# A two-layer hybrid decoder trunk: the heads' stage in steps of four wide products in place of three

## The chip, the cores and the metric

The kernel runs on one core of one Trainium2 chip. The metric is the device time of one launch in microseconds (us), as a median of several runs; lower is better. One of the executions was also profiled.

The engines are named as the profile names them: PE (TensorE, matrix products and transposes), PEld (its weight loads), DVE (VectorE), ACT (ScalarE), POOL (GpSimd) and SP (SyncE, which issues the DMAs).

## The reference

Input x is 1024 positions by 1024 channels, float32. Two layers follow each other, then a final RMSNorm. A layer normalizes x, multiplies it with one wide input matrix, and splits the columns among three causal token mixers, their gates, and three merge gates.

```
proj = rmsnorm(x) @ w_in
A:  a = conv31(a_val * sigmoid(a_glu)); y_a = silu(layernorm(a)) * silu(a_z)
B:  q, k, v = silu(conv4(qkv)), 8 heads of 128; q, k l2-normed; beta, decay per head
    o = gated_delta_rule(q, k, v, beta, decay);  y_b = rmsnorm(o) * silu(b_z)
C:  y_c = gelu(c_u) * (tril(W_s) layernorm(gelu(c_v)) + b) * silu(c_z)
x = x + (g0*(y_a @ a_proj) + g1*(y_b @ b_proj) + g2*(y_c @ c_proj)) @ w_out
```

with g0, g1 and g2 the sigmoids of the merge gates. The part that matters here is B. The gated delta rule goes through the positions in chunks. Within a chunk a lower triangular matrix made of keys, decay and beta is inverted; from chunk to chunk a state S of 128 by 128 is carried on:

```
v_new = u - w @ S        (u, w: the inverse applied to values and keys)
o     = q_dec @ S + qk @ v_new
S     = d * S + k_dec^T @ v_new
```

## The kernel before

**Data.** Everything is float32. A wide product keeps float32 accuracy by splitting both factors into a high and a low part and adding three passes (high by high, high by low, low by high), each a product of 128 by 128 by 512. They write `ps` tiles. The splits are an ACT copy and a POOL or DVE subtraction (lines 184 and 185). Products of one chunk (128 by 128) run as narrow float32 products; the profile lists two records for each.

**Stages of a layer.** First come some products, then `pairs`: the input projection in a scheme with seven block products for eight. The norms, the convolutions and the first two heads' beginnings run beside it. Then comes the heads' stage, which the change touches: TensorE has 16 more gate tiles to make (`plain`, of 48 wide products each, weights loaded and split ahead), then proj_c and proj_a, and between these wide products the eight heads run. The rest of proj_c and proj_a, proj_b and the output product follow.

**The heads' stage.** `interleave(lead, sides)` takes a leading generator, `feed`, whose every step emits three wide products (one k of one half, in `product`, line 257), and a list of side generators, each with a first step and a gap. After each step of the lead it advances those sides that are due. So the order of the text is woven out of positions that are written down by hand as AT_ constants. PE, ACT and DVE run this text in its order here (`manual_schedule`); POOL's and SP's orders are chosen by a planner. A period of 32 steps (PERIOD) belongs to each head, and head s starts from o = 32 s + 17. Sides are advanced in the order of the heads, and for a head in the order of the list. The yc splits come last.

The sides of a head, with the lines of their work:

- `head_load` issues the loads of q, k, v, of the decay row `gam` and of z (lines 736 and 753).
- `head_decay` makes a mask on POOL (line 789), then eight exponentials on ACT, one a step (line 794).
- `head_keys` transposes the keys (line 762, two blocks of four), copies them (ACT, line 777) and sums eight squares (ACT, line 780).
- `head_pairs` makes q by k (line 811) and k by k (line 830) for all chunks, two blocks of four each, with DVE products behind (lines 812, 833); between them DVE makes the small vector W (lines 815 to 820) while POOL scales kE (line 823) and takes a power (line 822). Then parts go out to DRAM and come back in another shape.
- `head_sub` is a DVE solve of 15 steps, a product (line 864) and a reduction (line 865) each, and `head_fetch` loads the result.
- `head_inv` widens the inverse from blocks of 16 to 128: six sets of small products (lines 923, 930, 946, 956 with 958, 968, 974) with ACT copies between them.
- `head_values` transposes q and v, two blocks of four each; ACT sums four squares behind each q block (line 891) and scales four copies behind each v block (line 901).
- `head_rec` is the recurrence over eight chunks, three steps a chunk. One step applies the inverse (line 1004), and ACT makes `vh` (line 1006) and squares an earlier output (line 1027). The next makes the state's and the output's products (lines 1012 and 1021), and DVE the new state (line 1017) and the output (line 1023). The third multiplies the state with keys and queries (lines 995 and 1000); DVE makes `rt` (line 997) and ACT a copy (line 1001).
- `head_out` takes a power and a product on POOL (lines 1047 and 1048), waits some steps, transposes the output (line 1055), multiplies on DVE (line 1057) and stores.

The recurrence and the inversion write tiles of `pr`, of which there are two in turn; transposes and pairs write `pa`, also two. The 24 units of SBUF that hold a head's tiles are handed out first in, first out.

A gate tile, when its 48 products are done, gets two tanh on ACT (lines 1156 and 1158), which are queued when the next tile's first product is emitted, and is stored.

```
sides.append((with_priority(late(lambda s=s: head_rec(s, r.E))), o + AT_REC[0], AT_REC[1]))
...
interleave(steps(feed, n * H + RAMP + EXTRA), sides)
```

Of the kernel before, what the change touches and what calls it, by code (L numbers as in the profile page):

```python
# [18 lines left out]
NT = 8  # L19
H = 8  # L20
# [5 lines left out]
PERIOD = 32  # L26
RAMP = 17
HEAD0 = 8
AT_LOAD = -29
AT_DECAY = -32  # L30
AT_KEYS = -21
AT_PAIRS = -19, 1.4
AT_SUB = 4, 1
AT_FETCH = 19
AT_INV = -6, 1.6
AT_VALUES = -8, 2.5
AT_REC = 11, 1
AT_OUT = 8, 3
N_LATE = 3
SPLIT_AT = {8: (10, 12), 4: (3, 5)}  # L40
REST_AT = 0
# [5 lines left out]
S_HEAD = -4, 1  # L47
S_NEXT = 50, 61, 77, 76, 74
STEP_US, IDLE_US, WIDE_US = 0.7, 1.5, 1.4
EXTRA = 2  # L50
AT_YC = -20
LAG_DMA, LAG_POOL = 4, 5
B_ENG = "Activation", "DVE"
# [17 lines left out]
def hybrid_trunk_kernel(ctx: ExitStack, tc: tile.TileContext, x, norm_g, w_in, a_dw, a_dw_b,  # L71
# [104 lines left out]
    ya_d, yc_d = (dr.tile([4, P, T], F32, name=f"y{nm}_d") for nm in "ac")  # L176
# [12 lines left out]
        for _ in g:  # L189
            pass  # L190

    def interleave(lead, sides):


        sides = [[g, first, gap] for g, first, gap in sides]
        i = 0
        for _ in lead:
            for sd in list(sides):
                while sd[1] <= i:
                    if next(sd[0], sides) is sides:  # L200
                        sides.remove(sd)
                        break
                    sd[1] += sd[2]
            i += 1
        while sides:
            for sd in list(sides):
                if next(sd[0], sides) is sides:
                    sides.remove(sd)

    def steps(g, n):  # L210
        for _ in range(n):
            if next(g, n) is n:
                return
            yield

    def chain(*gs):
        for g in gs:
            yield from g
# [27 lines left out]
    def product(w, rhs, kt, done, ahead, used=None):  # L246


        ps = psums()
        for k in range(kt):  # L250
            for h in range(2):
                if 2 * k + h in SPLIT_AT[kt]:
                    ahead()
                if 2 * k + h == REST_AT and rests:
                    rests.pop()()
                for i, (wi, ri) in enumerate(PASSES):
                    pe.matmul(ps[h], lhsT=w[wi][:, k, :], rhs=rhs(h, ri, k),  # L257
                              start=(k == 0 and i == 0), stop=(k == kt - 1 and i == 2))
                if used and h:
                    used(k)  # L260
                yield
        FW(*w)
        with tc.high_priority():
            rest = done(ps)
        if rest:
            rests.append(rest)

    rests = []

    def half_first(ws, rhs, kt, parts=1):  # L270


        pss = [psums() for _ in ws]
        n = HALF // parts
        for h in range(2):
            for p in range(parts):
                sl = slice(p * n, (p + 1) * n)
                for w, ps in zip(ws, pss):
                    for k in range(kt):
                        for i, (wi, ri) in enumerate(PASSES):  # L280
                            pe.matmul(ps[h][:, sl], lhsT=w[wi][:, k, :], rhs=rhs(h, ri, k)[:, sl],  # L281
                                      start=(k == 0 and i == 0), stop=(k == kt - 1 and i == 2))
                        yield pss
        for w in ws:
            FW(*w)
# [755 lines left out]
    def head_out(l, s):  # L1041
        o, zs = by_chunk(s.u["vn"]), s.u["z"]
        f = sm.tile([P, 8], F32, name="f", bufs=1)
        dve.tensor_scalar(out=f, in0=s.ssq, scalar1=EPS, scalar2=128.0 * EPS, op0=ALU.add, op1=ALU.mult)
        dve.scalar_tensor_tensor(out=f, in0=s.sso, scalar=1.0 / 128.0, in1=f, op0=ALU.mult, op1=ALU.add)
        fr = sm.tile([P, 8], F32, name="fr", bufs=1)
        pool.tensor_tensor(out=fr, in0=f, in1=mhalf, op=ALU.pow)
        pool.tensor_tensor(out=o, in0=o, in1=bc(fr, 2, P), op=ALU.mult)
        for _ in range(LAG_POOL):
            yield  # L1050
        c = cols["ong", l]
        for half in range(2):
            tp = pa.tile([P, HALF], F32, name="pa")
            for j in range(4):
                pe.transpose(tp[:, j * P:(j + 1) * P], o[:, half * 4 + j, :], ident)
            sl = slice(half * HALF, (half + 1) * HALF)
            dve.scalar_tensor_tensor(out=zs[:, sl], in0=tp, scalar=vec[:, c:c + 1], in1=zs[:, sl],
                                     op0=ALU.mult, op1=ALU.mult)
            yield
        sp.dma_start(out=yb_d[s.hd], in_=zs)  # L1060
        F(s.u["vn"], s.u["z"])
# [143 lines left out]
    def load_split(src, ks, name, ys, lag=0, gap=0, apart=0):  # L1205

        new = []
        for k in ks:
            hi, lo = U(name + "h", dt=F32R), U(name + "l", dt=F32R)
            sp.dma_start(out=lo.bitcast(F32), in_=src[k])  # L1210
            new.append((hi, lo))
            for _ in range(apart):
                yield
        for _ in range(lag):
            yield
        for hi, lo in new:
            split(lo.bitcast(F32), hi, lo, dve)
            ys.append((hi, lo))
            for _ in range(gap):
                yield  # L1220
# [70 lines left out]
    def layer(l, before, ws=None, parts=1):  # L1291
# [4 lines left out]
        pss = []  # L1296
# [105 lines left out]
        hs = [new_head(hd) for hd in range(H)]  # L1402
# [37 lines left out]

        def plain():
            br, m = order[n_gates]
            for i, pss in enumerate(half_first((w(),), h_rhs, 8)):
                if i in (4, 6):
                    w.ahead()
                yield
            use_gate_tile(br, m)(pss[0])()
            for br, m in order[n_gates + 1:]:
                yield from product(w(), h_rhs, 8, use_gate_tile(br, m), w.ahead)
            yield from proj_c(yc, mp, w)  # L1450
            yield from proj_a(ya, mp, w)
        mp, yc, ya, yb = [], [], [], []
        w = Weights([(w_part(l, C_GATE + br * D + m * P), 8) for br, m in order[n_gates:]] +
                    [(src[l][:, m * P:(m + 1) * P], kt) for src, kt in ((c_proj, 4), (a_proj, 4), (b_proj, 8))
                     for m in range(NT)])
        feed = plain()
        n, sides = PERIOD, [(second_head, 0, S_SECOND[1])]
        def side2(f, first):
            sides.append((late(f), first, 1))
        for hd, s in enumerate(hs):  # L1460
            o = hd * n + (RAMP if hd else HEAD0)
            def side(f, first, gap=1):
                sides.append((late(f), o + first, gap))
            sides.append((with_priority(late(lambda s=s: head_rec(s, r.E))), o + AT_REC[0], AT_REC[1]))
            if hd:
                if hd > 1:
                    side(lambda s=s: head_load(s, "kq"), AT_LOAD - n)
                    side(lambda s=s: head_load(s, "d"), AT_DECAY - LAG_DMA - n)
                    side(lambda s=s: head_decay(s, r), AT_DECAY - n)
                    side(lambda s=s: head_keys(s), AT_KEYS - n)  # L1470
                    side(lambda s=s: head_pairs(s, r), AT_PAIRS[0] - n, AT_PAIRS[1])
                side(lambda s=s: head_sub(s), AT_SUB[0] - n, AT_SUB[1])
                side(lambda s=s: head_load(s, "v"), AT_VALUES[0] - 8)
            if hd:
                side(lambda s=s: head_fetch(s), AT_FETCH - n)
            side(lambda s=s: head_inv(s), *AT_INV)
            side(lambda s=s: head_values(s), *AT_VALUES)
            if hd < H - 1:
                side(lambda s=s: head_load(s, "z"), AT_OUT[0] + n - 8)
                side(lambda s=s: head_out(l, s), AT_OUT[0] + n, AT_OUT[1])  # L1480
        with tc.manual_schedule(engines={getattr(mybir.EngineType, e) for e in B_ENG}):
            plain_steps = (len(order) - n_gates) * 16
            side2(lambda: load_split(yc_d, range(4), "yc", yc, 8, 3), plain_steps + AT_YC)
            interleave(steps(feed, n * H + RAMP + EXTRA), sides)
        run(head_load(hs[H - 1], "z"))
        left = plain_steps + 2 * 8 * NT - (n * H + RAMP + EXTRA)
        interleave(feed, [(head_out(l, hs[H - 1]), 5, 2), (load_split(ya_d, range(4), "ya", ya), left - 78, 1),
                          (load_split(yb_d, range(3), "yb", yb), left - 24, 1),
                          (load_split(yb_d, range(3, H), "yb", yb, apart=2), left - 6, 1)])
        mg, wo = {}, []  # L1490
        def used(k):
            F(*yb[k])
            wf = wr_pool.tile([P, 8, P], F32, name="wr").rearrange("p k c -> p (k c)")
            sp.dma_start(out=wf, in_=w_out[l][k * P:(k + 1) * P, :])
            hi, lo = U("woh", dt=F32R), U("wol", dt=F32R)
            with tc.high_priority():
                split(wf, hi, lo, pool if k in (3, 5, 7) else dve)
            wo.append((hi, lo))
# [71 lines left out]
    with tc.manual_schedule(engines={mybir.EngineType.PE}):  # L1570
        norms, ws = first_layer()
# [5 lines left out]
        for l in range(DEPTH):  # L1577
            before = layer(l, before, ws, 1 if l else 2)
            ws = None
# [28 lines left out]
```

## Time and profile before

| what | value |
|---|---|
| median of 3 runs | 2663.96 us (2663.27 to 2668.45) |
| profiled execution | 2663.31 us |
| its span, first to last instruction | 2661.5 us |
| PE busy | 2568.4 us, 97% |
| DVE busy | 1656.7 us, 62% |
| ACT busy | 1256.4 us, 47% |
| POOL busy | 1423.5 us, 53% |
| mean granted clock of PE | 0.991 |

The profile is of one execution. Busy shares are means over stages with different limits. Times in rows are microseconds from the span's start, means marked ns are nanoseconds. "out<-in" gives the tiles that an instruction writes and reads, and the number behind it the partitions by elements. A bracket behind a row of the timeline says how long the engine was idle before it and what ended that. Records of PE overlap, since products are pipelined: the time that a product takes from the engine is read from start to start.

### The profile page before, as it was taken

What the parts mean: (1) busy time and instruction counts of PE and PEld (TensorE: products, weight loads), DVE (VectorE), ACT (ScalarE), POOL (GpSimd) and SP (SyncE); (2) the same over time, 40 slices, a digit from 0 to 9 for tenths busy, and PEclk for the clock granted to TensorE, in tenths of its full rate; (3) what the DMA queues carried; (4) which work ended last, traced back from release to release, by engine and by line L of the source; (5) the groups of instructions that cost most, each with busy time, mean ns of one, the idle gap of its engine ahead of it and who ended that gap; (6) DMA issues with size and microseconds to landing.
All of it is one profiled execution on the core that took longest, in us unless ns stands there. A gap on an engine that the chain in (4) does not pass through costs nothing.

```text
span 2661.5 us, 42685 instructions
## 1 busy us (share of the span) xinstructions
PE 2568.4 (97%) x15963; PEld 2113.4 (79%) x15963; DVE 1656.7 (62%) x2934; ACT 1256.4 (47%) x2996; POOL 1423.5 (53%) x1144
## 2 busy tenths in 40 slices
PE   7899999999899999999999999999998999999998
PEld 6688888778688888788867888887787888877887
DVE  6698999756445454445276889997564545444442
ACT  4434434565466666322134343356554666652221
POOL 7867777768433332363167777776673333324520
PEclk9999999999999999999999999999999999999999
DMA  4122333534634445554312223343445444445432
GB/s 158 48 64 88 104 95 107 155 108 122 184 103 111 145 106 169 182 170 138 107 68 63 63 82 110 95 150 104 118 131 173 114 131 112 136 139 189 156 130 76
DMA packets 361636, 319.65 MB, mean 120 GB/s; under 512 B 98931, under 2 KB 313557, under 8 KB 360405
## 3 DMA queue, kind: packets, MB, share of 16 engines
q1 hardware_dynamic: 361428, 316.92, 39.5%
q8 instruction: 126, 2.06, 0.3%
q14 instruction: 82, 0.66, 0.1%
HBM read 221.12 MB, written 95.75 MB: 119 GB/s over the span
## 4 chain that ended last, share of the span: by engine, by line
PE 80%; DVE 6%; POOL 4%; ACT 4%; DMA 3%; issue 2%; SPq 0%; DVEq 0%; POOLq 0%; ACTq 0%
PE ps L357 36%; PE ps L257 24%; PE ps L1271 7%; DMA gam<-gc_d 2%; PE pa L762 1%; PE ps L281 1%; POOL S L185 1%; PE pr L1012 1%; PE pr L1004 1%; PE pr L995 1%; POOL st L298 1%; PE pr L1021 1%; DMA wr<-in_w_in_dram 1%; PE pa L811 1%; DVE nm L1084 1%
## 5 line engine op out<-in xcount | busy, mean ns | idle before, releaser
L185 POOL TENSOR_TENSOR S<-st,S 128x512 fp32r<-128x512 f32 x248 | 332.5, 1341 | 166.1 <-ACT S L184 165.7
L695 DVE SCALAR_TENSOR_TENSOR pr<-o,dwT,pr 128x512 f32<-128x512 f32 (+7 forms) x480 | 357.0, 745 | 10.6
L357 PE MATMUL ps<-hT,A 128*128 128x512 f32 x1488 | 363.5, 392 | 0.0
L185 POOL TENSOR_TENSOR wl<-wr,wh 128x512 fp32r<-128x512 f32 (+2 forms) x164 | 198.6, 1225 | 293.1 <-PE ps L257 138.7
L257 PE MATMUL ps<-hT,wh 128*128 128x512 f32 x960 | 334.4, 429 | 0.0
L373 DVE TENSOR_TENSOR o<-o,ps 128x512 f32<-128x512 f32 x430 | 286.2, 681 | 77.4 <-PE ps L357 66.2
L357 PEld LDWEIGHTS ps<-hT,A 128*128 128x128 f32 x1488 | 279.4, 189 | 58.5 <-issue 0.5
L184 ACT ACTIVATE S<-st 128x512 fp32r<-128x512 f32 x248 | 156.7, 632 | 338.3 <-PE ps L357 196.4
L185 POOL TENSOR_TENSOR A<-wr,A 128x512 fp32r<-128x512 f32 x186 | 253.0, 1361 | 22.3 <-ACT A L184 22.0
L695 DVE SCALAR_TENSOR_TENSOR pr<-o,cvT,pr 128x512 f32<-128x512 f32 (+3 forms) x288 | 213.1, 752 | 48.9 <-ACT pr L715 43.3
L257 PE MATMUL ps<-hT,wl 128*128 128x512 f32 x480 | 189.3, 394 | 0.0
L184 ACT ACTIVATE A<-wr 128x512 fp32r<-128x512 f32 x186 | 117.2, 630 | 143.6 <-PE ps L357 126.3
L357 PE MATMUL ps<-T,A 128*128 128x512 f32 x744 | 183.4, 393 | 0.9 <-POOL A L185 0.5
L357 PE MATMUL ps<-hT,S 128*128 128x512 f32 x744 | 183.7, 392 | 0.0
L357 PE MATMUL ps<-T2h,S 128*128 128x512 f32 x496 | 167.9, 396 | 5.7 <-ACT T2h L184 3.0
L357 PE MATMUL ps<-T3h,S 128*128 128x512 f32 x496 | 167.1, 395 | 4.1 <-ACT o L369 3.6
L357 PE MATMUL ps<-T1h,S 128*128 128x512 f32 x496 | 164.7, 391 | 0.0
L357 PEld LDWEIGHTS ps<-T,A 128*128 128x128 f32 x744 | 139.1, 189 | 31.3 <-ACT o L717 1.6
L184 ACT ACTIVATE wh<-wr 128x512 fp32r<-128x512 f32 (+2 forms) x164 | 85.6, 549 | 165.2 <-issue 123.5
L357 PEld LDWEIGHTS ps<-hT,S 128*128 128x128 f32 x744 | 138.1, 188 | 28.4 <-ACT o L717 0.7
L257 PEld LDWEIGHTS ps<-hT,wh 128*128 128x128 f32 x960 | 151.1, 190 | 11.6
L1271 PE MATMUL ps<-woh,mg 128*128 128x512 f32 x512 | 140.7, 391 | 0.0
(298 smaller groups left out, 5723.6 us busy)
## 6 DMA issues: line engine op xcount, KB each, us to landing
wr<-in_w_in_dram SPq DMA_DIRECT2D x160, 512.0 KB
g_d<-gth SPq DMA_DIRECT2D x32, 512.0 KB
g_d<-o SPq DMA_DIRECT2D x16, 512.0 KB
z_d<-o SPq DMA_DIRECT2D x16, 512.0 KB
v_d<-o SPq DMA_DIRECT2D x16, 512.0 KB
k_d<-o SPq DMA_DIRECT2D x16, 512.0 KB
q_d<-o SPq DMA_DIRECT2D x16, 512.0 KB
gam<-gc_d SPq DMA_DIRECT2D x16, 512.0 KB
```

What stands on the lines that cost most here:

```text
L184: act.activation(out=hi, in_=src, func=AF.Copy)
L185: lo_eng.tensor_tensor(out=lo, in0=src, in1=hi.bitcast(F32), op=ALU.subtract)
L257: pe.matmul(ps[h], lhsT=w[wi][:, k, :], rhs=rhs(h, ri, k), start=(k == 0 and i == 0), stop=(k == kt - 1 and i == 2))
L281: pe.matmul(ps[h][:, sl], lhsT=w[wi][:, k, :], rhs=rhs(h, ri, k)[:, sl], start=(k == 0 and i == 0), stop=(k == kt - 1 and i == 2))
L298: eng.tensor_tensor(out=out, in0=in0, in1=in1, op=ALU.subtract)
L357: pe.matmul(ps, lhsT=wt[:, wi, k, :], rhs=blk(nb, ri, k), start=(k == 0 and i == 0), stop=(k == 3 and i == 2))
L373: dve.tensor_tensor(out=out, in0=other, in1=ps, op=ALU.add)
L695: dve.scalar_tensor_tensor(out=acc[:, lo:], in0=x[:, h * HALF + lo - s:(h + 1) * HALF - s], scalar=taps[s - 1], in1=acc[:, lo:], op0=ALU.m ...
L762: pe.transpose(tp[:, j * P:(j + 1) * P], src[:, half * 4 + j, :], ident)
L811: pe.matmul(tp[:, j], lhsT=kT[:, n], rhs=qT[:, n], start=True, stop=True)
L995: pe.matmul(ks, lhsT=kT[:, n], rhs=st, start=True, stop=True)
L1271: pe.matmul(ps[h], lhsT=mg[hh, ri, k // 4][:, k % 4, off:off + P], rhs=wo[k][wi][:, h * HALF:(h + 1) * HALF], start=(k == 0 and i == 0), s ...
```

## The change

The generators of wide products now yield after every product and no longer after three. `grouped(feed, 4)` makes steps of four of them; `interleave` gets the size of a step and counts positions in wide products, so the AT_ constants keep their old unit of three. A side that is due twice within a step is advanced twice. The recurrence's gap becomes 4/3, that is one recurrence step in each step of four. EXTRA grows from 2 to 12, so that the loop holds the last recurrence. The loads, the decay, the keys and the pairs of heads 2 to 7 move back (to a later place) by 6, 3, 3 and 3 old steps, the values by 5, and the output by 2, with a gap of 2 in place of 3. The loop after it goes on in steps of three.

```diff
-AT_LOAD = -29
-AT_DECAY = -32
-AT_KEYS = -21
-AT_PAIRS = -19, 1.4
+AT_LOAD = -23
+AT_DECAY = -29
+AT_KEYS = -18
+AT_PAIRS = -16, 1.4
-AT_VALUES = -8, 2.5
-AT_REC = 11, 1
-AT_OUT = 8, 3
+AT_VALUES = -3, 2.5
+AT_REC = 11, 4 / 3
+AT_OUT = 10, 2
-EXTRA = 2
+EXTRA = 12
+STEP = 4
...
-    def interleave(lead, sides):
+    def interleave(lead, sides, size=3):
-        sides = [[g, first, gap] for g, first, gap in sides]
+        sides = [[g, 3 * first, 3 * gap] for g, first, gap in sides]
         i = 0
         for _ in lead:
             for sd in list(sides):
-                while sd[1] <= i:
+                while sd[1] <= i + 0.01:
...
-            i += 1
+            i += size
...
+    def grouped(g, size, n=None):
+        while n is None or n > 0:
+            for _ in range(size):
+                if next(g, g) is g:
+                    return
+            yield
+            n = n and n - 1
...
                 for i, (wi, ri) in enumerate(PASSES):
                     pe.matmul(ps[h], lhsT=w[wi][:, k, :], rhs=rhs(h, ri, k),
                               start=(k == 0 and i == 0), stop=(k == kt - 1 and i == 2))
-                if used and h:
-                    used(k)
-                yield
+                    if used and h and i == 2:
+                        used(k)
+                    yield
...
-            interleave(steps(feed, n * H + RAMP + EXTRA), sides)
+            n_steps = 3 * (n * H + RAMP + EXTRA) // STEP
+            interleave(grouped(feed, STEP, n_steps), sides, STEP)
         run(head_load(hs[H - 1], "z"))
-        left = plain_steps + 2 * 8 * NT - (n * H + RAMP + EXTRA)
-        interleave(feed, [(head_out(l, hs[H - 1]), 5, 2), ...
+        left = plain_steps + 2 * 8 * NT - n_steps * STEP // 3
+        interleave(grouped(feed, 3), [(head_out(l, hs[H - 1]), 5, 2), ...
```

`half_first`, which makes the stage's first gate tile, gets the same finer yield.

## Rows read from the trace of the kernel before

**Rows 1.** Windows: span; PE, PEld, DVE, ACT, POOL busy (instructions); clock; DMA.
```profile
838.07:883.22 45.15, 44.35 (x476) 36.89 (x475) 22.50 (x74) 29.94 (x105) 16.34 (x15) 1.00 0.49 128
741.00:1067.00 326.00, 318.58 (x3339) 263.60 (x3337) 160.68 (x510) 207.57 (x716) 107.83 (x99) 1.00 0.45 127
```

**Rows 2.** Waits of PE (total, times, longest): stage of layer 1; whole span.
```profile
PE pr L995 <- DVE st L1017: 2.7, 6, 0.7
...
PE pr L923 <- DVE sub L918: 10.1, 2, 5.5
```

**Rows 3.** Timeline of PE: start, length, engine, line, operation, tiles, records.
```profile
774.86 0.62 PE L257 MATMUL ps<-hT,wh 128*128 128x512 f32 x2
...
775.55 0.62 PE L257 MATMUL ps<-hT,wh 128*128 128x512 f32 x2
...
848.82 0.38 PE L995 MATMUL pr<-st,kT 128*128 128x128 f32 x2
...
849.96 0.42 PE L1004 MATMUL pr<-rt,zt 128*128 128x128 f32 x2
```

**Rows 4.** Timeline of all engines behind the keys' last square.
```profile
849.98 1.92 POOL L823 TENSOR_TENSOR kE<-kE,E 128x1024 f32<-128x1024 f32 x1 [0.15 <-ACT junk L780]
...
852.40 0.17 DVE L820 TENSOR_SCALAR Wn<-W 128x8 f32<-128x8 f32 x1
...
853.07 0.34 DVE L1017 SCALAR_TENSOR_TENSOR st<-st,E,pr 128x128 f32<-128x128 f32 x1
...
853.47 0.49 PE L995 MATMUL pr<-st,kT 128*128 128x128 f32 x2 [0.34 <-DVE st L1017]
```

**Rows 5.** Groups of DVE, 741 to 1067 us: count, busy us, mean ns, idle.
```profile
L1057 DVE SCALAR_TENSOR_TENSOR zT<-pa,vec,zT 128x512 f32<-128x512 f32 x12 | 9.0, 750 | 10.4 <-PE pa L1055 10.4
...
L185 DVE TENSOR_TENSOR ycl<-ycl,ych 128x1024 fp32r<-128x1024 f32 x4 | 6.3, 1580 | 6.3 <-ACT ych L184 6.2
```

**Rows 6.** Timeline of ACT at the keys.
```profile
841.54 0.39 ACT L794 ACTIVATE gam<-gam,ng 128x128 f32<-128x128 f32 x1
841.84 0.59 ACT L777 ACTIVATE kE<-pa 128x512 f32<-128x512 f32 x1
```

**Rows 7.** Timeline at the values' first block, and the gate's first tanh.
```profile
859.87 0.37 ACT L1006 ACTIVATE vh<-pr,W 128x128 f32<-128x128 f32 x1
...
860.84 0.60 PE L762 MATMUL pa<-ident,qT 128*128 128x128 f32 x4
...
861.54 0.28 ACT L891 ACTIVATE junk<-pa 128x128 f32<-128x128 f32 x1 [1.01 <-PE pa L762]
...
863.01 0.62 ACT L184 ACTIVATE wh<-wr 128x512 fp32r<-128x512 f32 x1
...
870.38 0.62 ACT L1156 ACTIVATE gth<-ps 128x512 f32<-128x512 f32 x1
```

**Rows 8.** Timeline of PE where the inversion follows the recurrence.
```profile
866.30 0.39 PE L1000 MATMUL pr<-st,qT 128*128 128x128 f32 x2
...
866.91 0.75 PE L923 MATMUL pr<-sub 32*32 32x32 f32 x64 [0.22 <-DVE rt L997]
```

**Rows 9.** Timeline of POOL and DVE at an output's product on POOL.
```profile
784.66 1.92 POOL L1048 TENSOR_TENSOR vn<-vn,fr 128x1024 f32<-128x1024 f32 x1
...
785.10 1.54 DVE L864 TENSOR_TENSOR sub<-sub 128x40 f32<-128x40 f32 x1
...
786.91 0.23 DVE L864 TENSOR_TENSOR sub<-sub 128x48 f32<-128x48 f32 x1
```

**Rows 10.** Timeline of PE behind the last yc split.
```profile
1066.73 0.49 PE L1004 MATMUL pr<-rt,zt 128*128 128x128 f32 x2 [1.33 <-DVE rt L997]
```

**Rows 11.** Timeline of SP and PE: a load of keys and its first transposes.
```profile
876.50 0.32 SPq L736 DMA_DIRECT2D kT<-k_d  x1
...
886.23 0.60 PE L762 MATMUL pa<-ident,kT 128*128 128x128 f32 x4
```

More of the change, by code (lines that the diff above doesn't have):

```diff
@@ L268, in hybrid_trunk_kernel, with half_first @@
     rests = []
-    def half_first(ws, rhs, kt, parts=1):
+    def half_first(ws, rhs, kt, parts=1, single=False):
         pss = [psums() for _ in ws]
@@ L282, in half_first @@
                                       start=(k == 0 and i == 0), stop=(k == kt - 1 and i == 2))
+                            if single and i < 2:
+                                yield pss
                         yield pss
@@ L1442, in plain @@
             br, m = order[n_gates]
-            for i, pss in enumerate(half_first((w(),), h_rhs, 8)):
-                if i in (4, 6):
+            for i, pss in enumerate(half_first((w(),), h_rhs, 8, single=True)):
+                if i in (12, 18):
                     w.ahead()
@@ L1483, in layer @@
             side2(lambda: load_split(yc_d, range(4), "yc", yc, 8, 3), plain_steps + AT_YC)
-            interleave(steps(feed, n * H + RAMP + EXTRA), sides)
+            n_steps = 3 * (n * H + RAMP + EXTRA) // STEP
+            interleave(grouped(feed, STEP, n_steps), sides, STEP)
         run(head_load(hs[H - 1], "z"))
-        left = plain_steps + 2 * 8 * NT - (n * H + RAMP + EXTRA)
-        interleave(feed, [(head_out(l, hs[H - 1]), 5, 2), (load_split(ya_d, range(4), "ya", ya), left - 78, 1),
+        left = plain_steps + 2 * 8 * NT - n_steps * STEP // 3
+        interleave(grouped(feed, 3), [(head_out(l, hs[H - 1]), 5, 2), (load_split(ya_d, range(4), "ya", ya), left - 78, 1),
                           (load_split(yb_d, range(3), "yb", yb), left - 24, 1),
```

## The prediction

> **What bounds the kernel now.** I read the page first (TensorE busy 97% of the span), then the windows, TensorE's waits and the timeline of the heads' stage, the only stage that the diff touches. TensorE sets the time there too: of 326.00 us from 741 to 1067 it is busy 318.58, and one period of a head takes 45.15 [rows 1]. Three wide products alone take 0.69 us (774.86 to 775.55), and the same three behind step C of the recurrence 1.14 (848.82 to 849.96) [rows 3]: 0.45 for two narrow products and nothing for the change between kinds. So fewer and larger groups save nothing by themselves; TensorE's work is the same before and after, and only its waits can change. I call the recurrence's steps A (L1004, then `vh` on ACT), B (L1012 and L1021, then the state on DVE) and C (L995 and L1000, then `rt` on DVE). TensorE's waits for them are small: L995 waits 2.7 us in six heads, once in each [rows 2]. That wait is the ceiling's main part.
>
> **The change part by part.** Offsets turn into places so: an offset x of head s falls 3(x+21) wide products after the first recurrence step of head s-1; divided by 4 and rounded up it is the step of four, 0 to 23, in which it comes. A is in steps 0, 3, 6 ..., B in 1, 4 ..., C in 2, 5 .... A gate tile ends every 48 products, so its two tanh are queued on ACT just ahead of steps 3 and 15. ACT, DVE and TensorE run this stage in the order of the text, so what stands ahead of `vh` or the state in the queue comes first. Step lengths from [rows 3, 7]: four wide products 0.93, A 0.22, B or C 0.45, four transposes 0.44 (their 0.60 less an overlap of 0.16), eight records of a pair 0.90 (the same way). Terms are for one layer; there are two.
>
> (a) Keys move from -21 to -18. Both blocks of transposes now fall in step 3 (9 and 12 over 4), the first pair product in step 4, two PSUM tiles between them. ACT has ahead of the first copy in step 3: two tanh (0.48 each from start to start, the row at 870.38 shows 0.62 with its tail), `vh` 0.37, a square 0.4 (1.47 for four), two exponentials 0.60 (841.54 to 841.84), then the copy 0.59 [rows 6, 7]: 2.9. TensorE is at the pair product 0.22+0.87+0.93+0.45 = 2.5 after step 3. Wait 0.3 (between 0, if ACT starts earlier, and 0.9 with a weight split between), for six heads: 1.8.
>
> (b) The end of the keys. In the rows of before GpSimd's product of kE starts at 849.98, 0.1 after the last square; DVE's small products for W end at 852.57 behind it, the state runs at 853.07 and L995 starts at 853.47 after 0.34 idle, some 0.55 late with the refill [rows 4]. After: before, the squares ended 8.0 us behind the start of the first copy (841.84 [rows 6] to 849.9); now that starts 2.2 behind step 3 and the copies stand together, so about 6.7 later, at 8.9. W ends 2.3 to 2.67 later, at 11.2. Now the half product of the output of head s-2 stands in step 7 ahead of the state (0.75 [rows 5]), then the state 0.35: 12.3. TensorE is at C of step 8 after 0.22+0.87+0.93, 0.45+0.3+0.9+0.93, 0.45+0.9+0.93, 0.22+0.93 and 0.44+0.45+0.9+0.93 (steps 3 to 7, (a)'s wait in) = 10.75. Late by 1.6 in place of 0.55: 1.05 for heads 3 to 7 and 0.3 for head 2, which has no output ahead: 5.6. Bounds: 0, if W's products slip in before kE's, and 6.6 with W at 2.67. I take 5.6, as the row has it.
>
> (c) Values move from -8 to -3: their first block of transposes falls in step 14 (54 over 4), its four squares just ahead of the two tanh and of `vh` in step 15. The block starts 1.5 after step 14 begins (C 0.45, wait for a PSUM tile 0.38, 64 small products 0.68), the first square 0.70 after it (860.84 to 861.54), the four take 1.47 (to 863.01), the tanh 0.96, `vh` 0.37 [rows 7] and 0.06 to the product behind it (as from 853.41, where the state ends, to 853.47 [rows 4]): 5.07. TensorE is at B of step 16 after 1.51+0.36+1.01 (step 14) and 1.16 (step 15) = 4.04. Wait 1.0, seven heads: 7.0. Before, the same squares stood two steps ahead of a `vh` and the tanh three behind. Between 0, if ACT did the tanh first, and 1.2 each with the refill.
>
> (d) The inversion stays at -6, but the recurrence of the head before now runs to step 22, so all its six products share a step with A, B or C; before, two did. Both use two PSUM tiles in turn: L923 behind C waits until `rt` has read the tile (866.30 to 866.91, 0.38 over the 0.22 that L1000 needs [rows 8]). After, steps 19 and 20 wait like this as well: 2 x 0.38, less some 0.18 that small tiles cost alone, less 0.2 for the wait that goes: 0.4, seven heads: 2.8. Between 0 and 5.3.
>
> (e) The four yc splits on ACT and DVE keep their products; with the recurrence of head 6 still running, the one at step 18 puts a DVE product (1.58 in the mean [rows 5]), behind its ACT copy, ahead of step 19's state: up to 2.7. Before, the last one made L1004 wait 1.33 [rows 10], which may go. I take 1.2 (between -1.5 and 2.7).
>
> (f) Head 0: TensorE waits for the first inversion in both layers, 10.1 us in all [rows 2]; two transposes that ran before it now come after: 0.9.
>
> (g) Gains: other waits of the recurrence, for which the extra product of 0.23 is cover: an estimate of 1.5 at most, taken whole. That 11 fewer groups remain in a period is worth 0 [rows 3].
>
> (h) Loads: keys are issued at 876.50 and transposed from 886.23, 9.7 us [rows 11]. Now their load stands at step 23, four steps or some 5 us ahead; SP can issue earlier, as the tile it takes was stored from at step 15. Cost 0; without that cover 2 us a head. The decay's and values' loads keep their distances in us. Output moves from 8 to 10 with a step of 2: behind the recurrence's end again, 0 on TensorE. EXTRA and the shorter rest move products from one loop to the next: 0.
>
> Sum: 1.8+5.6+7.0+2.8+1.2+0.9-1.5 = 17.8 a layer, 36 us. The profiled execution took 2663.31 (span 2661.5 and 1.8 around it), the median is 0.65 above: 2663.96+36 = 2700.
>
> **The rivals.** (1) Faster: the extra product covers every round trip and ACT and DVE absorb the rest. Then L995's waits (2.7 idle and six refills of 0.27), (g)'s 1.5 and (e)'s 1.5 go: 7.3 a layer, 2649. For it: ACT is busy 207.57 of 326.00 and DVE 160.68 [rows 1], so there is room on average; against it: (b) and (c) are queues at one place, not averages. (2) No change: gains and new waits cancel, 2664. (3) Slower still, by GpSimd: the output's product (1.92) moves from the gap between recurrences to steps 1 to 3. In the rows a DVE product of two SBUF tiles that takes 0.23 next to it took 1.54 while it ran [rows 9]; such a product now stands ahead of `rt` in step 2, which is then 1.4 late in six heads: 17 more, 2717. It decides if GpSimd starts before DVE. (4) Slower by late keys as in (h), 12 heads at 2: 2724.
>
> The Trainium skill bears on (3): SBUF — State Buffer, section "Who interferes with whom", says that a VectorE instruction with two inputs in SBUF contends with a GpSimd instruction that reads SBUF, and that whichever starts first holds the shared ports for its whole length. By that rule, the trace agrees (1.54 against 0.23), and by the rule alone the time would be rival 3's.
>
> **How the numbers follow.** Forecast 0.52 (2680 to 2715 on its own), rival 1 0.18, rival 2 0.10, rival 3 0.13, rival 4 0.07. A difference under 0.2% (5.3 us) cannot be told from none here. Faster 0.18, same 0.10, slower 0.72. The range 2652 to 2722 leaves out half of rival 1 and most of rival 4.
>
> **What would show it.** In the profile after: L1012 waiting for `vh` about 1 us once a period behind the squares L891 and the tanh (c); L995 waiting about 1.4 once a period (b); L811 waiting for the copy L777 (a); L956 and L968 waiting behind the recurrence (d); the period near 48 us in place of 45.15. Wrong if the period is under 45.15 with TensorE's waits fewer, if `vh` in step 15 does not stand behind the tanh, or if TensorE waits for loads of keys.

## The result and the profile after

The changed kernel takes 2712.52 us (median of 4 runs, 2711.73 to 2717.0) against 2664.23 of the kernel before on the same chip: ratio 1.0182, 95% interval 1.017 to 1.0194. The forecast was 2700, inside 2652 to 2722, and slower was the likeliest sign. The profiled execution has a span of 2711.4 us against 2661.5: 49.9 more. Some 2.4 of it arise in layer 1 before its heads' stage begins, where the change has no part (see (f) below); from the end of the first inversion on, the two layers take 23.7 and 23.9 more, where 17.8 a layer was forecast. Lines of the changed file stand 13 further down (those of the splits 1): A is L1017, B L1025 and L1034, C L1008 and L1013, `vh` L1019, the state L1028 or L1030, `rt` L1010. The inversion's six sets of products are called p0 (L936), q0 (L943), p1 (L959), q1 (L969 with L971), p2 (L981) and q2 (L987).

The windows of the kernel after: one interior period (from the start of the inversion's last product, L987, to the next head's), then the stage of layer 1. It answers to [rows 1].

```profile
843.23:890.76 47.53, 44.92 (x475) 37.89 (x474) 23.48 (x74) 29.83 (x106) 16.19 (x15) 1.00 0.45 121
741.00:1085.00 344.00, 320.63 (x3328) 268.72 (x3327) 160.27 (x501) 205.61 (x714) 102.80 (x97) 1.00 0.42 117
```

The period is 47.53 in place of 45.15 ("near 48" was forecast), with TensorE's busy time almost what it was (44.92 and 44.35): what came is waiting. TensorE's waits in the stage of layer 1 (us in total, times, longest) answer to [rows 2]:

```profile
PE pr L1025 <- ACT vh L1019: 7.5, 12, 0.9
PE pr L969 <- DVE st L1030: 4.1, 6, 3.0
PE pr L1008 <- DVE st L1030: 2.6, 3, 1.6
PE pr L1008 <- DVE st L1028: 2.0, 5, 0.4
...
PE pa L824 <- ACT kE L790: 1.4, 6, 0.6
PE pr L959 <- DVE sub L875: 1.0, 1, 1.0
```

Below, what a wait loses is the distance of TensorE's starts over the usual one, that is the idle time of the row and 0.1 to 0.17 of refill.

The timeline of ScalarE and TensorE in that period, at steps 12 to 13 and 15 to 16 (start, length, engine, line, operation, idle ahead of it and its releaser):

```profile
870.24 0.63 ACT L185 ACTIVATE wh<-wr 128x512 fp32r<-128x512 f32 x1
870.77 0.35 ACT L1019 ACTIVATE vh<-pr,W 128x128 f32<-128x128 f32 x1
...
871.18 0.49 PE L1025 MATMUL pr<-vh,kE 128*128 128x128 f32 x2 [0.38 <-ACT vh L1019]
...
876.09 0.28 ACT L904 ACTIVATE junk<-pa 128x128 f32<-128x128 f32 x1 [1.03 <-PE pa L775]
...
877.56 0.59 ACT L1169 ACTIVATE gth<-ps 128x512 f32<-128x512 f32 x1
878.03 0.60 ACT L1171 ACTIVATE gth<-ps 128x512 f32<-128x512 f32 x1
878.51 0.38 ACT L1019 ACTIVATE vh<-pr,W 128x128 f32<-128x128 f32 x1
...
878.95 0.49 PE L1025 MATMUL pr<-vh,kE 128*128 128x128 f32 x2 [0.87 <-ACT vh L1019]
```

The lower half is step (c) as forecast: the four squares (from 876.09), the two tanh, and only then `vh`, whose product A had been issued at 876.76; 1.03 lost. The upper half was not forecast: the copy of a gate weight's second part (L185) stands ahead of `vh` of step 12, 0.54 lost at B of step 13.

The start of the same period (GpSimd, VectorE, TensorE), not forecast either:

```profile
846.70 2.53 POOL L186 TENSOR_TENSOR wl<-wr,wh 128x512 fp32r<-128x512 f32 x2
...
846.88 1.13 DVE L1057 TENSOR_SCALAR f<-ssq 128x8 f32<-128x8 f32 x1
...
848.12 1.13 DVE L1058 SCALAR_TENSOR_TENSOR f<-sso,f 128x8 f32<-128x8 f32 x1
...
850.18 0.28 DVE L1028 COPY st<-pr 128x128 f32<-128x128 f32 x1
...
850.52 0.49 PE L1008 MATMUL pr<-st,kT 128*128 128x128 f32 x2 [0.42 <-DVE st L1028]
```

The output's two small products, eight columns each, take 1.13 each because each of them lies beside one of GpSimd's two products (2.53 for both); the state copy of step 1 stands behind them and C of step 2 loses 0.58. This is rival 3's mechanism at another place. Its own place was harmless: the product beside the output's (1.75 at 851.31) came behind `rt`.

Step (b): VectorE's first product for W and GpSimd's product of kE, in the same period and in that of head 6:

```profile
861.02 0.17 DVE L828 TENSOR_SCALAR nk<-ssk 128x8 f32<-128x8 f32 x1 [1.41 <-ACT junk L793]
```
```profile
865.80 1.92 POOL L836 TENSOR_TENSOR kE<-kE,E 128x1024 f32<-128x1024 f32 x1
```
```profile
1003.72 1.92 POOL L836 TENSOR_TENSOR kE<-kE,E 128x1024 f32<-128x1024 f32 x1 [8.04 <-ACT junk L793]
...
1003.75 1.92 DVE L828 TENSOR_SCALAR nk<-ssk 128x8 f32<-128x8 f32 x1 [1.41 <-ACT junk L793]
...
1006.23 0.75 DVE L1070 SCALAR_TENSOR_TENSOR zT<-pa,vec,zT 128x512 f32<-128x512 f32 x1
1006.89 0.34 DVE L1030 SCALAR_TENSOR_TENSOR st<-st,E,pr 128x128 f32<-128x128 f32 x1
...
1007.28 0.49 PE L1008 MATMUL pr<-st,kT 128*128 128x128 f32 x2 [1.57 <-DVE st L1030]
```

At 1007.28 everything is as priced (W stretched, the output's half, the state; 1.74 lost). In four of the six periods GpSimd has other work first, its product of kE comes 4 to 6 us later (865.80), W's product takes 0.17, and C of step 8 loses at most 0.09. At the keys (a), the copies (L790) make the first pair product, L824, lose 0.33 (0.3 was forecast).

Step (e), behind the first yc split:

```profile
1073.50 1.23 DVE L186 TENSOR_TENSOR ycl<-ycl,ych 128x1024 fp32r<-128x1024 f32 x1 [4.64 <-ACT ych L185]
1074.64 0.34 DVE L1030 SCALAR_TENSOR_TENSOR st<-st,E,pr 128x128 f32<-128x128 f32 x1
...
1075.04 0.22 PE L969 MATMUL pr<-sub 32*32 32x32 f32 x2 [2.97 <-DVE st L1030]
```

It is not C that waits for the late state but the inversion's product q1 (L969), one step earlier: it takes the PSUM tile that the state has still to read, so the four wide products of the step are no cover. 3.14 lost where 1.2 was forecast. Behind this wait the granted clock is 0.59 from 1075 to 1078 (last section), and four wide products there start 0.43 us and more apart in place of 0.23: some 1.0 more.

### The profile page after: what moved, and what is told of

Its sections match the earlier page's. It is cut to its first block, busy times and chain, and to the rows that moved or that the text cites. A ratio compares the mean times of both kernels' runs of the same rounds, so it can differ in the third digit from the quotient of the medians.

```text
span 2711.4 us, 42725 instructions
## 1 busy us (share of the span) xinstructions
PE 2580.4 (95%) x15963; PEld 2128.9 (79%) x15963; DVE 1661.3 (61%) x2934; ACT 1256.8 (46%) x2996; POOL 1425.1 (53%) x1144
## 5 line engine op out<-in xcount | busy, mean ns | idle before, releaser
L185 ACT ACTIVATE S<-st 128x512 fp32r<-128x512 f32 x248 | 156.6, 631 | 339.8 <-PE ps L370 193.2
L268 PE MATMUL ps<-hT,wl 128*128 128x512 f32 x480 | 200.3, 417 | 0.0
L268 PEld LDWEIGHTS ps<-hT,wh 128*128 128x128 f32 x960 | 174.3, 190 | 24.0
L185 ACT ACTIVATE A<-wr 128x512 fp32r<-128x512 f32 x186 | 117.2, 630 | 143.9 <-PE ps L370 126.3
L185 ACT ACTIVATE wh<-wr 128x512 fp32r<-128x512 f32 (+2 forms) x164 | 86.5, 551 | 165.7 <-issue 120.6
```

The costliest lines, as they stand in the source:

```text
L185: act.activation(out=hi, in_=src, func=AF.Copy)
L268: pe.matmul(ps[h], lhsT=w[wi][:, k, :], rhs=rhs(h, ri, k), start=(k == 0 and i == 0), stop=(k == kt - 1 and i == 2))
```

## The experiments

The edits are on the changed kernel unless said. Ratios are to the kernel before, with 95% intervals, and differences between kernels are differences of these ratios times 2664 us; periods are interior ones of layer 1 (heads 2 to 5).

**e1_values.** `AT_VALUES = -3, 2.5` becomes `-2, 2.25` (its load's offset 8 becomes 9).

> The changed kernel with the values' first block of transposes one step later (15 in place of 14, behind `vh` and not ahead of it; the other three blocks and the load stay in their steps). Theory of queues at places: only step (c) goes, TensorE's wait of 1.03 us at B of step 16, seven times a layer, so 14 us less: 2698. Rival 1, the longer recurrence in groups of four costs by itself and a wait removed comes back in another step: 2709 to 2713. Rival 2, GpSimd's products cost the time: 2712, unchanged.

Measured 2711.01 (2704.41 to 2714.45), ratio 1.0175 (1.0157 to 1.0194). The profiled execution took 2704.41, at a mean clock of 0.990; the other three ran at 0.985 to 0.987 (the changed kernel at 0.988 to 0.990), and in total the kernel can't be told from the changed one. By place it can: TensorE's wait for `vh` in a period falls from 1.2 in two waits to 0.4 in one (B of step 13), and the period from 47.5 to 46.8. Part came back: p1 (L959) now waits 0.3 for ScalarE. How much of the total the lower clock of the three other executions took was not separated.

**e2_keys_order.**

```
+        ke = sm.tile([P, 8], F32, name="ke", bufs=2)
+        dve.tensor_copy(out=ke, in_=E[:, 1, :, hd])
-        pool.tensor_tensor(out=kE, in0=kE, in1=bc(E[:, 1, :, hd], 2, P), op=ALU.mult)
+        pool.tensor_tensor(out=kE, in0=kE, in1=bc(ke, 2, P), op=ALU.mult)
```

> The changed kernel with GpSimd's product of kE made to wait for the end of W: VectorE copies the eight factors behind W and the product reads the copy. Theory of queues at places: W's small products no longer stretch beside it, so the waits of L1008 at C of step 8 (1.05 and 1.74 us, in two periods of each layer) go, 5.6 us less: 2707; the copy itself costs 0.2 or less where it stands ahead of a state, nothing on TensorE. Rival, step (b) is the output's half product ahead of the state and not GpSimd: unchanged, 2712, and the two waits stay.

Measured 2707.65 (2705.99 to 2710.93), ratio 1.0167 (1.0152 to 1.0183). W's first product of head 6 takes 0.17, C of step 8 waits no more, that period is 47.64 in place of 49.3 and head 0's 52.3 in place of 53.5. By these places the size is as forecast (2.8 a layer); the total falls by 4.0, with a last period of layer 2 that ran 2.5 longer at half the clock (last section). The rival is out: the output's half ahead of the state costs nothing alone.

**e3_bank.** One PSUM tile for a step's two narrow products.

```
         def ptile():
-            return pr.tile([P, HALF], F32, name="pr")[:, 0:P]
+            t = pr.tile([P, HALF], F32, name="pr")
+            return t[:, 0:P], t[:, P:2 * P]
```

> The changed kernel with the two narrow products of a recurrence's step in one PSUM tile (columns 0 to 127 and 128 to 255) in place of two, so that a step takes one of the two tiles in turn and the inversion's product behind it finds the other free. Theory of shared tiles (step (d)): the waits of p0 and q0 (0.38 each), q1 (0.38), p2 (0.28) and the 0.09 beside them go, 1.4 us in each of seven periods, two layers: 20 us less, 2693, if nothing else is late then; TensorE comes 0.8 earlier to B of step 16, whose `vh` does not come earlier, so a part may come back there: down to 2704. Rival, the waits are for the readers' data and not for the tile: 2712.

Measured 2890.65 (2890.11 to 2894.32), ratio 1.0857 (1.0839 to 1.0876): neither theory's. The timeline at one step B:

```profile
935.23 0.38 PE L1025 MATMUL pr<-vh,kE 128*128 128x128 f32 x2
935.65 0.35 DVE L1030 SCALAR_TENSOR_TENSOR st<-st,E,pr 128x128 f32<-128x128 f32 x1 [1.95 <-PE pr L1025]
936.05 0.49 PE L1033 MATMUL pr<-vh,qk 128*128 128x128 f32 x2 [0.44 <-DVE st L1030]
```

The second product now waits for the reader of the first, though it writes other columns: 0.61 or more lost in every B and C. The Trainium skill, PSUM — Partial Sum Buffer, section "PSUM bank collisions raise a hardware error", has a reason for such a wait: two engines may not be in one bank of a partition at once, whatever the columns. That it was put in for this reason here, no run shows. It came with the edit, and f_bank2 takes it out.

**f_bank2.** The same tile, both products issued ahead of the first reader.

> The changed kernel with the two narrow products of a recurrence's step in one PSUM tile, as in e3_bank, but with both products ahead of the first reader, so that the second no longer waits for the reader of the first. Theory of shared tiles (step (d)): the waits of p0, q0 and q1 (0.38 each), of p2 (0.28) and the 0.09 beside them go, 1.3 us a period; TensorE then comes 0.76 earlier to B of step 16, whose `vh` comes no earlier, so 0.5 to 0.6 a period stays, 8 us in all: 2704, and L1025's wait in step 16 grows to about 1.7. Rival, readers that now start one product (0.1 to 0.2) later lose at each step more than that: 2712 to 2730.

Measured 2698.25 (2695.47 to 2701.49), ratio 1.0125 (1.0108 to 1.0141): 15 less than the changed kernel, twice the forecast. The waits of p0, q0, q1 and p2 are gone, the period is 46.65, and `vh` at step 13 loses 0.70 in place of 0.54 (at 16 it stays at 1.03, not 1.7). The last period shows most, 42.8 in place of 46.4: the yc split is as before, but q1 no longer waits, C behind the four wide products loses 1.59, and the clock does not fall behind it.

```profile
1066.40 1.23 DVE L186 TENSOR_TENSOR ycl<-ycl,ych 128x1024 fp32r<-128x1024 f32 x1 [4.55 <-ACT ych L185]
1068.03 0.46 PE L1009 MATMUL pr<-st,kT 128*128 128x128 f32 x2 [1.44 <-DVE st L1032]
```

So (d) holds, and the shared tile is what made (e) dear.

**e4_size3.** `STEP = 4` becomes 3, `AT_REC = 11, 4 / 3` becomes `11, 1`: what is left of the change are the moved offsets (the output's gap and EXTRA among them).

> The changed kernel with steps of three wide products and the recurrence one step of three apart again (24 of the period's 32), all other offsets as changed: keys and values later by the same part of a period. Theory of queues at places: the blocks fall elsewhere (keys' copies in steps 3 and 4 of 32, values' squares behind `vh` of step 18), so (a), (c) and the shared tiles of q1 and p2 go: 2668, between 2660 and 2680. Rival, the later keys and values are what costs, wherever the recurrence stands: 2695 to 2712. Rival, only the stretched recurrence costs: 2664, the same as the kernel before.

Measured 2654.5 (2652.22 to 2656.76), ratio 0.9966 (0.9953 to 0.9979): faster than the kernel before by 9, and under the forecast's lower end by 5. Together the moves cost nothing, they gain; one by one they were not run. Its period:

```profile
878.32:923.34 45.02, 44.23 (x475) 37.17 (x474) 22.28 (x74) 30.06 (x105) 16.22 (x16) 1.00 0.48 128
```

**f_stretch.** `STEP = 3` alone; the recurrence still takes the whole period.

> The changed kernel with steps of three wide products, and the recurrence still one step every four products (it takes all of the period), all offsets as changed. Theory of queues at places: in steps of three the recurrence's steps fall 0, 2, 3, 4, 6, 7, ..., so that two steps lie between A and B, and tanh, squares or splits ahead of `vh` make no wait; shared tiles cost 0.3 to 0.5 a period: 2662, between 2655 and 2675. Rival 1, the recurrence over the whole period costs: 2700 or more, as with groups of four. Rival 2, only the group of four costs: 2655, as e4_size3.

Measured 2676.87 (2673.27 to 2680.57), ratio 1.0042 (1.0026 to 1.0058); the forecast's upper bound is missed by 2, both rivals by more. An interior period costs only 0.5:

```profile
884.42:929.90 45.48, 44.57 (x475) 37.79 (x475) 24.59 (x74) 29.62 (x105) 16.20 (x15) 1.00 0.49 126
```

Its loss on e4_size3 stands at the edges: from the first inversion's end to the last's it takes 321.9 in place of 315.7 in layer 1 and 323.1 in place of 315.4 in layer 2, half of it in head 0's period (52.6 in place of 49.4, 53.8 in layer 2); what makes that period long was not tested. With e4_size3 this splits the change, in this order of steps: the moves give 9 us, the stretch takes 20, the groups of four take 37.

**f_mend.** e1_values', e2_keys_order's and f_bank2's edits, and `AT_OUT = 10, 2` becomes `9.35, 2`.

> The changed kernel in steps of four with four places mended together: values' first block one step later (e1_values, 8.4 less by its profile), kE's product behind W (e2_keys_order, 4 less), one tile for a step's two products (f_bank2), and the output's two small products one step earlier, in step 23 behind the end of the recurrence and two steps ahead of the state copy that they held up (C of step 2, 0.58 in five periods of a layer, 0.44 in one: 6.6 less). Theory of queues at places: the sum, about 27 less: 2685, a period of 45.6 to 46. Rival, in steps of four a wait that is removed comes back at the next step: 2700 to 2710.

Measured 2694.52 (2692.29 to 2697.97), ratio 1.0109 (1.0094 to 1.0124): 19 less, not 27. The period is 46.36. The waits that were mended are gone (C of step 2, B of step 16, the tiles), but `vh` still makes B of step 13 lose 0.71, L824 loses 0.71 in place of 0.33, and A (L1019 in this file) 0.35, the product of k by k (L845) 0.40 and p1 (L961) 0.45 are new. Theory and rival are both partly right: about a third comes back.

**g_split.** `SPLIT_AT[8] = 10, 14` in place of `10, 12` while the gate's products run.

> The changed kernel with a gate weight's second split on ScalarE later by two of the product's sixteen places, in step 13 of four in place of 12 (and the one that fell in step 0 in step 1), behind `vh` and not ahead of it. Theory of queues at places: TensorE's wait of 0.54 at B of step 13 goes in six periods of a layer: 6 us less, 2706. Rival, the copies of the inverse's blocks and not the split make this `vh` late, or the wait comes back at step 16: 2711 to 2714.

Measured 2703.29 (2700.44 to 2714.52), ratio 1.0148 (1.0129 to 1.0167): 9 less. (The profiled execution is the longest of the four, 2714.52 at a mean clock of 0.983, the others at 0.989 and 0.990; it is read for places alone.) The wait at B of step 13 went, and that of C of step 2 with it; the period is 46.38. The start of that period:

```profile
893.97 1.29 POOL L186 TENSOR_TENSOR wl<-wr,wh 128x512 fp32r<-128x512 f32 x1
894.16 1.12 DVE L1057 TENSOR_SCALAR f<-ssq 128x8 f32<-128x8 f32 x1
895.40 0.17 DVE L1058 SCALAR_TENSOR_TENSOR f<-sso,f 128x8 f32<-128x8 f32 x1
...
897.21 0.38 PE L1008 MATMUL pr<-st,kT 128*128 128x128 f32 x2
```

The second of the two splits is no longer there, so the output's second product takes 0.17 in place of 1.13, and C does not wait. One weight's split made both waits that the prediction had not priced.

**g_shift.** `AT_REC = 11 - 4 / 3, 4 / 3` and `AT_OUT = 8.01, 2`: the recurrence one step of four earlier.

> The changed kernel in steps of four with the recurrence one step (four products) earlier, step A in steps 23, 2, 5, ... and the output's start two steps earlier, in step 22 behind the recurrence's end; all else as changed. Theory of phase: a gate tile is twelve steps of four, a multiple of the recurrence's three, so that in the changed kernel both tanh and a weight's split stand ahead of `vh` in every period; one step earlier they stand in B's steps, where ScalarE has nothing that TensorE waits for. So the waits of B at steps 13 and 16 (0.54 and 1.03) and of C at step 2 (0.58) go, some 2 us a period and 28 in all; new may be values' second squares ahead of `vh` in step 17 and the output's second half ahead of `rt` in step 7 (0.2 to 0.5 each), shared tiles as before: 2690, between 2678 and 2700. Rival, groups of four cost by themselves, wherever the recurrence stands: 2707 or more.

Measured 2698.98 (2695.72 to 2701.59), ratio 1.0123 (1.0109 to 1.0137): 16 less, at the end of the range and under the rival's bound. C of step 2 waits no more and `vh` at most 0.4, but in one period p0 (L936) waits 1.3 (0.7 and 0.5 in the next two): `rt`, whose tile it shares, stands on VectorE behind the inversion's first transpose, which waits for its load. The place counts; this one has its own collisions. Its clock is lower too, 0.982 to 0.987, where the changed kernel has 0.988 to 0.990: in each layer, at a wait of 2.5 at q1, the granted clock fell to 0.50 for 13.65 us (1061.67 to 1075.32 in layer 1). So the total may hold back some of what the place gave; how much was not separated.

**g_phase.** f_stretch with `AT_REC = 11 + 1 / 3, 4 / 3`.

> f_stretch (steps of three, the recurrence one step every four products) with the recurrence later by a third of an offset, so that the step left free comes ahead of A and not behind it: A in steps 1, 5, 9, ..., B right behind in 2, 6, ... Theory of phase: the tanh of steps 4 and 20 now stand ahead of `vh` in steps 5 and 21 with one step of cover in place of two, those of step 5 with the keys' two copies and exponentials as well: 1 to 2 us late each, and the first steps' splits 0.3: some 3 us a period, 2715, between 2695 and 2730. Rival, the stretch and the size of a step set the time and the place in the period does not: 2677, as f_stretch.

Measured 2687.04 (2684.86 to 2688.74), ratio 1.0076 (1.0061 to 1.0092): 9 more than f_stretch. The sign is right and the rival is out, the size a quarter of what I forecast. A period is 46.2, and `vh` makes B lose 0.32 and 0.36, not 1 to 2. At the first of the two, ScalarE gets through an exponential and one of the keys' copies (899.54 and 899.83) before A is issued at 900.27; the tanh, an exponential and the second copy do stand ahead of `vh` (900.31 to 902.03), but B's cover takes most of that. At the second it is not the tanh that stands there but two copies of L857 (913.08).

**f_best2.** e4_size3 with f_bank2's and e2_keys_order's edits.

> e4_size3 (steps of three, recurrence one step of three apart, later loads, keys and values) with one PSUM tile for a recurrence step's two products, both ahead of their readers, and kE's product behind W. Theory of shared tiles: p0's and q0's waits (0.38 each) go in seven periods of each layer, 10 us less than e4_size3: 2644. Rival, readers that start one product later lose as much: 2654 or more.

Measured 2658.69 (2656.67 to 2662.78), ratio 0.9975 (0.9963 to 0.9987), not told apart from e4_size3: the rival. p0 and q0 wait no more, but `vh` ahead of them makes B lose 0.63 in place of 0.48 and the period is 44.95.

**g_best.** e4_size3 with `AT_PAIRS = -16, 1.3` in place of 1.4.

> e4_size3 with the pair products' spacing at 1.3 in place of 1.4, so that the second copies of the diagonal blocks leave step 14 of 32, where a weight's split stands with them ahead of `vh` in step 15, for step 13. Theory of queues at places: the only larger wait left in its period, 0.48 at B of step 16, goes or shrinks to 0.1: 0.4 in six or seven periods of each layer, 5 us less: 2649 against 2654.5 of e4_size3. Rival, the split alone makes `vh` late: 2654.

Measured 2655.25 (2650.37 to 2656.57), ratio 0.9956 (0.9944 to 0.9969). B of step 16 in e4_size3, and then here:

```profile
905.10 0.49 PE L1025 MATMUL pr<-vh,kE 128*128 128x128 f32 x2 [0.32 <-ACT vh L1019]
```
```profile
906.85 0.41 PE L1025 MATMUL pr<-vh,kE 128*128 128x128 f32 x2
```

The wait is gone and the period 44.47, but head 0's period is 50.4 in place of 49.4, so that from the first inversion's end to the last's only 1.2 is left in layer 1 and 1.7 in layer 2, and the total can't be told from e4_size3's. Either of the two beats both kernels.

## Why the prediction was right, and where it was not

The sign and its reason held: TensorE's work is the same, and new waits at single places of ScalarE's and VectorE's queues outweigh what longer groups give. By terms of one layer (lost us; measured from the starts in layer 1, from the end of the first inversion on; (g) is what is left of the sum):

```
term                           forecast  measured
(a) keys' copies                    1.8       2.4
(b) W, output's half, state         5.6      -0.7
(c) squares and tanh                7.0       7.2
(d) shared tiles                    2.8       2.5
C of step 2, B of step 13             -       6.1
(e) yc splits, last recurrence      1.2       6.7
(f) head 0                          0.9       1.1
(g) the rest                       -1.5      -1.6
sum                                17.8      23.7
```

(c) is exact (seven waits of 1.03); e1_values takes the wait away, by place and not in the total. (a) and (d) hold in place and nearly in size. (a)'s own times give 0.4 a head (2.9 less 2.5) and not the 0.3 that I wrote, so 2.4, which is what came. Two figures beside the sum are off as well: (b)'s upper bound with W at 2.67 comes to some 7.5, not 6.6, and rival 1's six waits of L995 cost 3.5 by the starts, not the 4.3 of 2.7 and six refills of 0.27.

(b) failed in the sentence that took W's end from the rows of before: there GpSimd's product of kE started 0.1 behind the last square [rows 4], and I carried this order over. After, it does so in two periods (1.05 and 1.74 lost, 2.8), while the six waits of L995 (3.5 with their refills) went. e2_keys_order shows the cause.

Two waits were missing, 2.8 and 3.3 a layer. I had gone through what stands ahead of `vh` only in the steps with tanh, and ahead of the state only in step 7; the split of a weight in steps 12 and 0 (on ScalarE, and on GpSimd beside the output's products) is the same argument at a place where I had not made it. g_split shows both. By chance they stand for what (b) lacked, so the interior period came out near the forecast (2.4 longer) for reasons of which half were wrong.

(e) failed in its upper bound of 2.7. I priced the state's delay at C and its cover, and did not put it together with (d): a product that shares the tile waits without cover. f_bank2 shows it: 1.59 lost in place of 3.14. The last recurrence, with three more splits beside it, lost 6.6 after the last inversion, 4.0 before. The remaining 1.0 of (e) is no wait but the lower clock behind one; no term of the prediction had the clock.

(f) has its size by chance. Its own wait did not grow: p0 waits 9.8 for the first inversions of both layers, 10.1 before. The 1.1 is p1 ahead of head 1, which loses 1.14 behind VectorE's start on the next head's blocks (L875), which I had not looked at. The first inversion of layer 1 ends 2.5 later, but 2.3 of it are there at 567 us, ahead of the heads' stage, and 1.4 of these came at one place behind a wait that both kernels have, where the clock fell in one of them (last section); in layer 2 the way from the layer's start to the first inversion's end is as long as before (754.2 and 754.3).

Rival 1's condition, that the cover absorbs all, is refuted; rival 3's mechanism struck, but ahead of the state copy of step 1 and not ahead of `rt` of step 2, for 2.8 a layer in place of 8.5. The Trainium skill, SBUF — State Buffer, section "Who interferes with whom", says that whichever starts first has the shared ports for its whole instruction and the other is blocked; the rows agree (1.13 beside products of 1.27, and 1.92 beside 1.92, each time with GpSimd first). Rival 4 did not come: no wait for loads of keys shows.

What stays open: with four places mended, groups of four still cost 18 us more than f_stretch. The remaining waits are 0.3 to 0.7 each at five places, and I did not take them away one by one, so I can't say whether some order in steps of four would be as fast as in steps of three. Nor is the stretch's 20 us taken apart.

## What to carry to other kernels

Where engines work through queues in a written order, price a new period by going through every instruction ahead of each link of the recurrence, in every step, and not only the ones that were moved; with a period of twelve steps to a tile and three to a round, the same neighbours meet each time. Two effects at one place (a late reader and a shared buffer) are priced together: the shared buffer takes the cover away. Test the parts of a change apart: here one of three parts gained 0.34% and the other two lost 2.2%. When two profiles are compared, first see where the difference begins: 2.3 us of this one stood ahead of the stage that was changed.

## What the hardware showed that I had not expected

TensorE's clock can fall behind a single wait, and the wait then costs more than its own length. Windows of the kernel after, around the wait at 1075.04 (columns as in [rows 1], the clock third from the end):

```profile
1071.00:1075.00 4.00, 1.06 (x7) 0.79 (x5) 1.50 (x3) 2.44 (x6) 0.00 (x0) 1.00 0.49 131
1075.00:1078.00 3.00, 2.96 (x54) 2.51 (x55) 0.18 (x1) 1.12 (x3) 0.00 (x0) 0.59 0.00 0
1078.00:1090.00 12.00, 11.10 (x77) 8.80 (x76) 4.46 (x9) 7.38 (x18) 3.47 (x3) 0.96 0.71 264
```

and of e2_keys_order behind the same wait in layer 2:

```profile
2406.50:2416.00 9.50, 9.38 (x86) 7.94 (x87) 0.50 (x2) 3.53 (x11) 0.00 (x0) 0.50 0.47 147
```

The granted clock there is 0.50 of full speed, the lower of the two levels, for 9.5 us, and that period is 48.85 in place of 46.34 in layer 1. Around the waits of 1 us of the period shown first, the clock stays at 1.00.

The length of the wait alone does not tell. Ahead of the stage both kernels have the same wait of 2.90; before, the clock stayed at 1.00 behind it, after, it fell:

```profile
531.03 0.66 PE L1097 MATMUL pa<-ident,acc 128*128 128x128 f32 x4 [2.90 <-ACT acc L1118]
531.00:536.00 5.00, 4.97 (x28) 4.08 (x28) 3.16 (x8) 4.42 (x11) 1.85 (x2) 1.00 0.26 107
```
```profile
532.05 0.66 PE L1110 MATMUL pa<-ident,acc 128*128 128x128 f32 x4 [2.90 <-ACT acc L1131]
532.80:536.30 3.50, 3.50 (x10) 2.72 (x9) 1.99 (x6) 3.50 (x10) 1.66 (x2) 0.51 0.37 152
```

And in g_phase it fell behind a wait of 1.43 at p1 (788.83): 0.51 from 789.50 to 793.00. Executions of one kernel with a lower mean clock also took longer: of e1_values, 2704.41 at 0.990 and 2714.45 at 0.985.
